# Holding back filler products in a state space stage: every gate block queued behind a step's output products

## The chip, the cores and the metric

The kernel runs on one core of a Trainium2 chip. The metric is the device time of one execution in microseconds (us). A core has TensorE (PE in the profile; its weight loads are PEld), VectorE (DVE), ScalarE (ACT), GpSimd (POOL) and SyncE (SP), each with a queue of its own that it works through in order, and DMA queues. The ones used here are issued by SP, ScalarE and GpSimd.

## The reference

Two layers of a streaming encoder over 2048 prompt positions and 8 x 16 sample positions, 1024 wide. Layer 0 is a diagonal complex state space mixer (S5), layer 1 a gated delta rule mixer. The change lies in layer 0:

```python
proj = h @ w_in
u, z = jnp.split(proj, 2, axis=-1)
...
# 64 groups of 16 channels, 64 complex states each
br = jnp.einsum('gpc,btgc->btgp', bbr, uc)
bi = jnp.einsum('gpc,btgc->btgp', bbi, uc)
...                                  # x_t = Abar x_{t-1} + Bbar u_t, state carried
y = jnp.einsum('gcp,btgp->btgc', c_re, xr) - jnp.einsum('gcp,btgp->btgc', c_im, xi)
...
y = jax.nn.gelu(y + d.astype(F32) * uf)
y = y * jax.nn.sigmoid(y @ w_glu.astype(F32) + b_glu.astype(F32))
y = y * jax.nn.silu(z.astype(F32))
return y.astype(h.dtype) @ w_out, hr, hi
```

The gate z is used only behind the whole scan, so its product with the second half of `w_in` may be computed at any time until then.

## The kernel before, in words

All 2176 positions stand in 8 column tiles of 272. A float32 product is made as three reduced-precision products of a high and a low part (`mm3`, L149 to L151), 24 matmuls for one output block of 128 x 272. Four stages matter here.

1. The projection to u (tile pd), which also leaves h in memory (`h0_d`).
2. The state space stage, 16 steps b, each for 4 groups. `s5_setup(b)` makes the step's matrices on VectorE, with transpositions (abT, L682) and small products (pk, L698) on TensorE. `s5_main(b)` makes input products (pb, L735, two sets of 8 matmuls), turns them (f, z) and scans them (L749) on VectorE, turns the states back (t, xs, L763 to L766), splits them into a high part on ScalarE (xsh, L129) and a low part on VectorE (xsl, L130), and makes the output products py. For each of two halves pl there are two PSUM tiles, py_0 and py_1 for the first, py_2 and py_3 for the second: a Toeplitz product each (L775) and six products with the states each (L780). The L780 products read 64 rows: one tile's use the upper half of TensorE's rows, the other's the lower half (`tile_position`). ScalarE applies the activation to y and stores it (`y_d`).
3. The gate blocks: 64 calls of `z_block`, block n being row block cb = n % 8 of column tile j = n // 8. Each makes one `mm3` into one of two PSUM buffers (pdz), which ScalarE copies out (evz, L630) and stores. Their input is read back from `h0_d` (hz), half a column tile at a time, and split into hhz on ScalarE and hlz on VectorE. They stand in the code behind the 16 steps.
4. The next stage, which loads y (yc), splits it (yh, yl), loads and splits the weights wg (into the buffers of the gate's weights), and makes pg.

The order of each engine's queue isn't the order of the code. A scheduler builds it: an instruction that is ready may stand ahead of code that waits, so gate blocks fill TensorE's time between the steps' products. Two things bind it: data and buffers, and `issue_after`, which the helper `later` uses: instructions traced under it stand, in the queue of the named instruction's engine, behind that instruction. `s5_main` returns `ends`, the last output matmul of each half. Before, only the blocks from 58 on are bound: block 58 to the first half of step 15, blocks 59 to 63 to the second.

Of the kernel before, what the change touches and what calls it, by code (L numbers as in the profile page):

```python
# [41 lines left out]
def bc(ap, axis, n):  # L42
    a = ap.unsqueeze(axis)
    shape = list(a.shape)
    shape[axis] = n
    return a.broadcast_to(shape)


def dram_ap(t, offset, dims):
    return bass.AP(t.tensor, t.offset + offset, [list(d) for d in dims])  # L50
# [3 lines left out]
def kernel(ctx: ExitStack, tc: tile.TileContext, I, O, upto="Z"):  # L54
# [73 lines left out]
    def split_w(dst_hi, dst_lo, raw, lo_eng=None):  # L128
        S.copy(dst_hi, raw)  # L129
        (lo_eng or V).tensor_sub(dst_lo, raw, dst_hi.bitcast(F32))  # L130
# [9 lines left out]
    def later(ins):  # L140
        st = ExitStack()
        for i in ins:
            st.enter_context(tc.issue_after(i))
        return st
# [462 lines left out]
    zst = {"n": 0}  # L607
# [11 lines left out]
    def z_block():  # L619
        j, cb = divmod(zst["n"], 8)  # L620
        zst["n"] += 1
        if cb == 0:
            zst["cur"] = zst.pop("next")
        if cb == 2 and j < 7:
            zst["next"] = load_h0(j + 1)
        hh, hl = zst["cur"]
        ps = psd.tile([P, NCH], F32, tag="d", name=f"pdz{j}_{cb}")
        mm3(ps, ks(wz_hi[cb]), ks(wz_lo[cb]), hh, hl)
        o = ev.tile([P, NCH], F32, tag="o", name=f"evz{j}_{cb}")
        S.copy(o, ps)  # L630
        nc.scalar.dma_start(z_d[j][cb], o)
# [3 lines left out]
    with ExitStack() as pb:  # L635
# [28 lines left out]
        def s5_setup(b):  # L664
            sp = b3.tile([P, SPW], F32, tag="sp", bufs=2, name=f"sp_{b}")
            nc.sync.dma_start(sp, sp_d[b])
            pw = sp[:, PWO:BBO].rearrange("p (l r n) -> p l r n", l=2, r=3)
            bbv = sp[:, BBO:BDO].rearrange("p (r l c) -> p r l c", r=2, l=2)
            bdv = sp[:, BDO:CCO].rearrange("p (r l m) -> p r l m", r=2, l=2)
            ccv = sp[:, CCO:SPW].rearrange("p (r l c) -> p r l c", r=2, l=2)  # L670

            abt = b1.tile([P, 2, 2, 8, 16], F32, tag="abt", name=f"abt{b}")
            tt = b1.tile([P, 2, 2, 9, 16], F32, tag="tt", name=f"abtt{b}")
            for l in range(2):
                V.tensor_mul(abt[:, l], bc(bc(bbv[:, 0, l], 1, 8), 1, 2), bc(pw[:, l, 0:2, 0:8], 3, 16))
                V.tensor_mul(tt[:, l, :, 0:8], bc(bc(bbv[:, 1, l], 1, 8), 1, 2), bc(pw[:, l, 1:3, 0:8], 3, 16))
            V.tensor_add(abt.rearrange("p l r n c -> p (l r) (n c)"), abt.rearrange("p l r n c -> p (l r) (n c)"),
                         tt.rearrange("p l r n c -> p (l r) (n c)")[:, :, 0:128])
            ab = b2.tile([P, 4, P], F32, tag="ab", name=f"ab{b}")
            pt = ps_t.tile([P, 4, P], F32, tag="t", name=f"abT{b}")  # L680
            for q in range(4):
                T.transpose(pt[:, q, :], abt[:, q // 2, q % 2].rearrange("p n c -> p (n c)"), ident)  # L682
            S.copy(ab, pt)

            ca = b3.tile([P, 2, 2, 9, 16], F32, tag="ca", bufs=2, name=f"ca{b}")
            t2 = b1.tile([P, 2, 2, 9, 16], F32, tag="tt", name=f"cat{b}")
            for l in range(2):
                V.tensor_mul(ca[:, l], bc(bc(ccv[:, 0, l], 1, 9), 1, 2), bc(pw[:, l, 1:3], 3, 16))
                V.tensor_mul(t2[:, l], bc(bc(ccv[:, 1, l], 1, 9), 1, 2), bc(pw[:, l, 0:2], 3, 16))
            V.tensor_sub(ca, ca, t2)  # L690
            cs_ = [b2.tile([P, 2, 2, P], F32R, tag="ca" + i, name=f"ca{i}{b}") for i in "hl"]
            split_w(*(t.rearrange("p l r (n c) -> p (l r) n c", c=16) for t in cs_),
                    ca[:, :, :, 1:9].rearrange("p l r n c -> p (l r) n c"))

            pk = ps_t.tile([P, P], F32, tag="t", name=f"pk{b}")
            for l in range(2):
                for r in range(2):
                    T.matmul(pk[32 * l:32 * l + 32, :], lhsT=bdv[:, r, l],  # L698
                             rhs=ca[:, l, r, 0:8, :].rearrange("p n c -> p (n c)"), start=(r == 0), stop=(r == 1),
                             tile_position=(0, 32 * l))  # L700
            kp = b2.tile([64, 240], F32, tag="kp", bufs=1, name=f"kp{b}")
            G.memset(kp[:, 0:112], 0.0)
            S.copy(kp[:, 112:240], pk[0:64])
            V.scalar_tensor_tensor(kp[:, 112:128], dmask, d16[:, b:b + 1], kp[:, 112:128], op0=ALU.mult, op1=ALU.add)
            nc.scalar.dma_start(k_d[b], kp)
            toe = b2.tile([P, 4, P], F32, tag="toe", name=f"toe{b}")
            for g in range(4):
                nc.sync.dma_start(toe[:, g, :], dram_ap(k_d[b], 16 * g * 240, [[16, 8], [240, 16], [1, P]]))
            return cs_, ab, toe

        def s5_load(b):
            u = b2.tile([P, 4, NCH], F32, tag="ur", name=f"u{b}")
            nc.sync.dma_start(u.rearrange("p g c -> p (g c)"),
                              dram_ap(u_d[b // 2], 4 * (b % 2) * NCH, [[8 * NCH, P], [1, 4 * NCH]]))
            tw = b2.tile([P, 2, 2, SEG], F32, tag="tw", name=f"tw_{b}")
            nc.sync.dma_start(tw, tw_d[b])
            return u, tw

        def s5_main(b, u, tw, ca, ab, toe):
# [67 lines left out]
                    y.rearrange("p g c -> p (g c)"))  # L787
            return ends

        par = s5_setup(0)  # L790
        ld = s5_load(0)
        for b in range(16):
            nxt = (s5_load(b + 1), s5_setup(b + 1)) if b < 15 else None
            ends = s5_main(b, *ld, *par)
            if nxt:
                ld, par = nxt
        V.tensor_sub(fsp[:, :, 0], fe[:, 0, :, 0], fe[:, 1, :, 1])
# [8 lines left out]
            zst["next"] = load_h0(0)  # L806
        while zst["n"] < 64:

            with later([ends[zst["n"] > 58]] if zst["n"] > 57 else []):
                z_block()  # L810
    pab.close()
    if upto == "B":
# [472 lines left out]
    with pd:  # L1285
# [457 lines left out]
        par = es.tile([P, 2], F32, name="par")  # L1743
# [329 lines left out]
def _build(arrays, upto="Z"):  # L2073
    import concourse.bacc as bacc

    nc = bacc.Bacc("TRN2", target_bir_lowering=False, num_devices=1)
    I = {k: nc.dram_tensor("in_" + k, v.shape, F32, kind="ExternalInput").ap() for k, v in arrays.items()}
    O = {k: nc.dram_tensor("out_" + k, s, F32, kind="ExternalOutput").ap() for k, s in _OSHAPE.items()}
    with tile.TileContext(nc, schedule_with_timeline_sim=True) as tc:
        dbg = kernel(tc, I, O, upto)  # L2080
    return nc, dbg
# [9 lines left out]
```

## Time and profile before

| what | value |
|---|---|
| three runs | 2153.47, 2156.33, 2158.28 us; median 2156.33 |
| the profiled execution | 2155.81 us |
| its span | 2154.1 us |
| PE busy | 2087.0 us, 97% |
| DVE busy | 1566.3 us, 73% |
| ACT busy | 972.4 us, 45% |
| POOL busy | 476.7 us, 22% |
| pdz matmuls | 512 each of three kinds, first start 272.2, last 619.1 |
| py matmuls | first start 289.9, last 602.4 |

A row of the timeline has the start in us, the length, the engine, line, operation, tiles (output<-inputs), shape and count; what stands in brackets is the engine's idle time before it and what ended that. A row of a window has for each engine the busy us and, in parentheses, the number of instructions that touch the window, then the granted TensorE clock (PEclk, 1.00 is full speed), the share of DMA time and the rate. A row of a group ends with its busy us, the mean length in ns, and the idle time before. A row of waits has total, number and longest.

### The profile page before, as it was taken

The numbers are of one execution on the slowest core, as the hardware profiler recorded it, in microseconds if no ns is written. First come the engines' busy times: TensorE is split into PE (matmuls) and PEld (weight loads), VectorE is DVE, ScalarE is ACT, GpSimd is POOL, SyncE is SP. The second block draws the span as 40 slices with busy tenths as digits, with TensorE's granted clock in tenths as the row PEclk, the third lists the DMA queues.
The fourth block names the chain that finished last, engine by engine and source line by source line (L and its number), as shares of the span: only waits on it lengthen the run. The fifth ranks groups of instructions, "written<-read, shape, count | busy, mean of one in ns | idle before, by whom it ended". The sixth has DMA issues, their size and how long they took to land. (4 is left out here: it accounts for less than half of the span.)

```text
span 2154.1 us, 42178 instructions
## 1 busy us (share of the span) xinstructions
PE 2087.0 (97%) x15729; PEld 1852.0 (86%) x15729; DVE 1566.3 (73%) x4013; ACT 972.4 (45%) x2289; POOL 476.7 (22%) x725
## 2 busy tenths in 40 slices
PE   6999999999889999999999999999999899999998
PEld 4889888888689999999888879889987788888887
DVE  7999598999856554446765669688556888888875
ACT  3543333333255444446665422341224556666663
POOL 1157510000113222222100000100011343444430
PEclk8999999999889999999999999999999899999999
DMA  9697844454284333336465313653456644444432
GB/s 278 238 307 242 250 146 133 145 172 145 93 242 136 126 111 109 110 99 213 139 204 173 93 48 86 163 145 101 137 165 217 195 141 134 124 139 147 146 112 69
DMA packets 395209, 332.40 MB, mean 154 GB/s; under 512 B 88026, under 2 KB 358890, under 8 KB 395004
## 3 DMA queue, kind: packets, MB, share of 16 engines
q1 hardware_dynamic: 259084, 226.56, 35.3%
q10 hardware_dynamic: 133104, 95.49, 13.8%
q0 software_dynamic: 2816, 7.65, 1.0%
q8 instruction: 124, 2.03, 0.4%
q14 instruction: 81, 0.66, 0.1%
HBM read 213.01 MB, written 116.61 MB: 153 GB/s over the span
## 5 line engine op out<-in xcount | busy, mean ns | idle before, releaser
L149 PE MATMUL pc<-h1h,wdh 128*128 128x512 f32 (+1 forms) x600 | 216.5, 361 | 0.1
L151 PE MATMUL pc<-h1h,wdl 128*128 128x384 f32 (+1 forms) x600 | 214.9, 358 | 0.0
L150 PE MATMUL pc<-h1l,wdh 128*128 128x384 f32 (+1 forms) x600 | 214.8, 358 | 0.1
L1404 DVE SCALAR_TENSOR_TENSOR ac<-pb,convw,ac 128x384 f32<-128x384 f32 (+3 forms) x288 | 163.5, 591 | 3.3
L150 PE MATMUL pdz<-hlz,wzh 128*128 128x272 f32 x512 | 152.4, 298 | 0.0
L149 PE MATMUL pdz<-hhz,wzh 128*128 128x272 f32 x512 | 151.6, 297 | 0.7 <-ACT evz L630 0.7
L149 PE MATMUL pg<-yh,wgh 128*128 128x272 f32 x512 | 148.2, 289 | 3.5 <-ACT evz L630 3.5
L151 PE MATMUL pdz<-hhz,wzl 128*128 128x272 f32 x512 | 150.9, 295 | 0.0
L149 PE MATMUL po<-gh,woh 128*128 128x272 f32 x512 | 148.2, 290 | 1.4 <-ACT gh L937 1.4
L150 PE MATMUL pg<-yl,wgh 128*128 128x272 f32 x512 | 149.1, 291 | 0.0
L151 PE MATMUL pg<-yh,wgl 128*128 128x272 f32 x512 | 148.2, 290 | 0.0
L151 PE MATMUL po<-gh,wol 128*128 128x272 f32 x512 | 147.9, 289 | 0.0
L150 PE MATMUL po<-gl,woh 128*128 128x272 f32 x512 | 147.1, 288 | 0.0
L149 PEld LDWEIGHTS pc<-h1h,wdh 128*128 128x128 f32 x600 | 112.6, 188 | 12.4 <-issue 1.7
L150 PEld LDWEIGHTS pc<-h1l,wdh 128*128 128x128 f32 x600 | 112.7, 188 | 10.4 <-issue 0.8
L151 PEld LDWEIGHTS pc<-h1h,wdl 128*128 128x128 f32 x600 | 112.6, 188 | 10.2 <-issue 0.8
L149 PE MATMUL pd<-hh,wuh 128*128 128x272 f32 x384 | 112.7, 294 | 0.1
L69 PE MATMUL epo<-w2h,ohi 128*128 128x512 f32 x272 | 111.5, 410 | 0.0
L150 PE MATMUL pd<-hl,wuh 128*128 128x272 f32 x384 | 110.8, 289 | 0.3 <-DVE hl L230 0.3
L151 PE MATMUL pd<-hh,wul 128*128 128x272 f32 x384 | 110.9, 289 | 0.0
L69 PE MATMUL epo<-w2h,olo 128*128 128x512 f32 x272 | 106.9, 393 | 0.0
L69 PE MATMUL epo<-w2l,ohi 128*128 128x512 f32 x272 | 106.8, 393 | 0.0
(617 smaller groups left out, 6334.5 us busy)
## 6 DMA issues: line engine op xcount, KB each, us to landing
wa<-in_w_ada SPq DMA_DIRECT2D x32, 512.0 KB
wdr<-in_w_in SPq DMA_DIRECT2D x24, 512.0 KB
h_d<-x ACTq DMA_DIRECT2D x8, 1088.0 KB
u_d<-ev ACTq DMA_DIRECT2D x64, 136.0 KB
hz<-h_d SPq DMA_DIRECT2D x16, 544.0 KB
u<-u_d SPq DMA_DIRECT2D x16, 544.0 KB
z_d<-evz ACTq DMA_DIRECT2D x64, 136.0 KB
y_d<-y ACTq DMA_DIRECT2D x32, 272.0 KB
```

Of the source, the lines that this page charges most:

```text
L69: i_ = f(*a, **kw)
L149: T.matmul(ps, lhsT=w_hi[k], rhs=x_hi[k], start=(k == 0), stop=False)
L150: T.matmul(ps, lhsT=w_hi[k], rhs=x_lo[k], start=False, stop=False)
L151: i_ = T.matmul(ps, lhsT=w_lo[k], rhs=x_hi[k], start=False, stop=(k == n - 1))
L1404: V.scalar_tensor_tensor(o, src(j), convw[:, b, j:j + 1], o, op0=ALU.mult, op1=ALU.add)
```

## The change

The last matmuls of all steps are kept, 32 in number (index 2b + pl), and each gate block is bound to one of them:

```diff
+        ends = []
         par = s5_setup(0)
         ld = s5_load(0)
         for b in range(16):
             nxt = (s5_load(b + 1), s5_setup(b + 1)) if b < 15 else None
-            ends = s5_main(b, *ld, *par)
+            ends += s5_main(b, *ld, *par)
             if nxt:
                 ld, par = nxt
...
         while zst["n"] < 64:
 
-            with later([ends[zst["n"] > 58]] if zst["n"] > 57 else []):
+            n = zst["n"]
+            step = 2 * (n * 15 // 52) - 1 if n < 52 else 29 if n < 58 else 30 + (n > 58)
+            with later([ends[step]] if step > 0 else []):
                 z_block()
```

Blocks 0 to 3 are free. Blocks 4 to 51 go 3 or 4 each behind the second half of steps 0 to 13, blocks 52 to 57 behind that of step 14, and the last six stay as they were. Names below carry the number of the step (py5_2), or of column tile and row block (pdz0_4 is block 4, pdz7_0 is block 56).

TensorE's queue from the second input product of step 0 on, before:

```order
L735 MATMUL pb0_1_4217<-u0_4153,ab0_4120 64x272 x4
L150 MATMUL pdz0_4_6407<-hlz0_0_6274,wzh4_4026 128x272
L698 MATMUL pk1_4188<-ca1_4177,sp_1_4161 32x128 x4
L775 MATMUL py0_0_4252<-u0_4153,toe0_4148 128x272
L775 MATMUL py0_1_4253<-u0_4153,toe0_4148 128x272
L151 MATMUL pdz0_4_6407<-hhz0_0_6273,wzl4_4027 128x272
```

and in the changed kernel:

```order
L735 MATMUL pb0_1_4217<-u0_4153,ab0_4120 64x272 x4
L775 MATMUL py0_0_4252<-u0_4153,toe0_4148 128x272
L698 MATMUL pk1_4188<-ca1_4177,sp_1_4161 32x128 x4
L775 MATMUL py0_1_4253<-u0_4153,toe0_4148 128x272
L682 MATMUL abT2_4305<-ident_160,abt2_4297 128x128 x4
L735 MATMUL pb1_0_4342<-u1_4157,ab1_4170 64x272 x4
L698 MATMUL pk2_4322<-ca2_4311,sp_2_4295 32x128 x4
L682 MATMUL abT3_4439<-ident_160,abt3_4431 128x128 x4
L735 MATMUL pb1_1_4351<-u1_4157,ab1_4170 64x272 x4
L780 MATMUL py0_0_4252<-xsh0_4247,cah0_4134 128x272
```

The gate blocks are gone from here until step 0's last output product (160 gate matmuls stood in this stretch before).

TensorE's queue at the second half of step 5's output products, before:

```order
L775 MATMUL py5_2_4942<-u5_4693,toe5_4734 128x272
L775 MATMUL py5_3_4943<-u5_4693,toe5_4734 128x272
L780 MATMUL py5_2_4942<-xsh5_4917,cah5_4720 128x272
L780 MATMUL py5_3_4943<-xsh5_4917,cah5_4720 128x272
L780 MATMUL py5_2_4942<-xsl5_4918,cah5_4720 128x272
L780 MATMUL py5_3_4943<-xsl5_4918,cah5_4720 128x272
```

and in the changed kernel:

```order
L775 MATMUL py5_2_4942<-u5_4693,toe5_4734 128x272
L780 MATMUL py5_2_4942<-xsh5_4917,cah5_4720 128x272
L780 MATMUL py5_2_4942<-xsl5_4918,cah5_4720 128x272
L780 MATMUL py5_2_4942<-xsh5_4917,cal5_4721 128x272
L780 MATMUL py5_2_4942<-xsh5_4917,cah5_4720 128x272
L780 MATMUL py5_2_4942<-xsl5_4918,cah5_4720 128x272
L780 MATMUL py5_2_4942<-xsh5_4917,cal5_4721 128x272
L775 MATMUL py5_3_4943<-u5_4693,toe5_4734 128x272
L780 MATMUL py5_3_4943<-xsh5_4917,cah5_4720 128x272
```

The two tiles' products no longer alternate. It is so in steps 0, 2 to 12 and 14 (in step 11 for the first five); before it was so in step 14 alone.

ScalarE's queue behind step 15's last activation, before:

```order
L785 DMA y_d_119<-y15_1_6235 128x544
L631 DMA z_d7_78<-evz7_2_8016 128x272
L135 CAST wgh3_8176<-wgr3_8254 128x1024
L630 COPY evz7_3_8044<-pdz7_3_8019 128x272
L631 DMA z_d7_78<-evz7_3_8044 128x272
L900 CAST yh0_0_8232<-yc0_0_8230 128x1088
L630 COPY evz7_4_8072<-pdz7_4_8047 128x272
```

and in the changed kernel:

```order
L230 CAST hhz7_1_7763<-hz7_1_7761 128x1088
L785 DMA y_d_119<-y15_1_6235 128x544
L630 COPY evz6_7_7932<-pdz6_7_7907 128x272
L631 DMA z_d6_77<-evz6_7_7932 128x272
L903 CAST yh0_0_8232<-yc0_0_8230 128x1088
L135 CAST wgh0_8182<-wgr0_8242 128x1024
L630 COPY evz7_0_7960<-pdz7_0_7935 128x272
L903 CAST yh0_1_8238<-yc0_1_8236 128x1088
```

The cast of y and that of the first weights now stand ahead of the copy of block 56 (evz7_0), and a split of the gate's input ahead of y's last store.

## The prediction

> **What bounds the kernel now.** I read the page first, for the engines by slice.
>
> ```profile
> span 2154.1 us, 42178 instructions
> PE   6999999999889999999999999999999899999998
> PEclk8999999999889999999999999999999899999999
> ```
>
> TensorE (PE) is full nearly everywhere, so its time is the kernel's: work that it doesn't do in a hole must be done later. The change lies in the state space stage, so I cut that stage by windows at the landmarks: z blocks begin (272.19), the fourth block ends (287.10), the products of step 0 end (318.92), the z blocks that may run ahead are used up (568.38), the first half of step 15's products ends (595.95), step 15 ends (602.69), the next stage begins (622.91).
>
> ```profile
> core 0: us, PE busy (x) PEld busy (x) DVE busy (x) ACT busy (x) POOL busy (x), PEclk, DMA share, GB/s
> 287.10:318.92 31.82, 31.82 (x254) 27.26 (x252) 31.13 (x75) 10.51 (x24) 0.48 (x3) 1.00 0.40 121
> 318.92:568.38 249.46, 248.04 (x1901) 205.67 (x1901) 223.01 (x469) 86.54 (x215) 3.63 (x25) 1.00 0.46 146
> 568.38:595.95 27.57, 16.31 (x66) 9.91 (x64) 23.68 (x37) 4.74 (x11) 7.42 (x8) 0.58 0.26 89
> 595.95:602.69 6.74, 6.74 (x41) 6.15 (x39) 2.45 (x2) 2.67 (x4) 0.00 (x0) 0.69 0.69 191
> 602.69:622.91 20.22, 15.97 (x124) 15.38 (x123) 7.79 (x7) 9.94 (x15) 0.00 (x0) 1.00 0.83 250
> ```
>
> Up to 568 PE has no idle time to speak of (248.04 of 249.46); VectorE has some (223.01). From 568.38 to 595.95 there is no z block left for PE: a hole, and a granted clock of 0.58. The same windows for the z blocks' tile alone:
>
> ```profile
> 287.10:318.92 31.82, 22.88 (x162) 20.52 (x160) 2.71 (x7) 1.00 0.40 121
> 318.92:568.38 249.46, 164.17 (x1136) 146.17 (x1136) 18.14 (x47) 1.00 0.46 146
> 568.38:595.95 27.57, 0.16 (x2) 0.00 (x0) 0.39 (x1) 0.58 0.26 89
> 602.69:622.91 20.22, 15.97 (x122) 15.38 (x122) 2.27 (x6) 1.00 0.83 250
> ```
>
> A z block is 24 matmuls. Their price is the distance between starts, not the listed length, since they overlap; these are 22 rows apart:
>
> ```profile
> 609.12 0.28 PE L150 MATMUL pdz<-hlz,wzh 128*128 128x272 f32 x1
> 611.87 0.29 PE L151 MATMUL pdz<-hhz,wzl 128*128 128x272 f32 x1
> ```
>
> So 2.75 / 22 = 0.125 us each, 3.0 us a block. In the long window 1136 of them are 142 us; the other 106 us are 13 steps of state space work, 8.1 us of PE each. VectorE is busy 223.01 / 13 = 17.2 us a step.
>
> **The change, term by term.** No instruction is added; 60 of 64 z blocks wait in PE's queue for a step's products. I keep a ledger of PE time up to the next stage's first matmul (after it PE is full, and a shift there stays).
>
> *(a) The late hole is filled: a gain.* What PE does from 568.38 to 595.95 at full clock: the products of step 14 in part, two input products of step 15, half of step 15's output products. Full clock prices, and the half-clock rows for the form that exists only there:
>
> ```profile
> L735 PE MATMUL pb<-u,ab 128*64 128x272 f32 x208 | 32.2, 406 | 1.4 <-DMA u<-u_d 1.4
> 565.20 1.08 PE L775 MATMUL py<-u,toe 128*128 128x272 f32 x4
> 566.21 0.39 PE L780 MATMUL py<-xsh,cah 64*128 64x272 f32 x2
> 567.15 0.39 PE L149 MATMUL pdz<-hhz,wzh 128*128 128x272 f32 x1
> 578.11 0.43 PE L780 MATMUL py<-xsh,cal 64*128 64x272 f32 x2
> 578.33 0.43 PE L780 MATMUL py<-xsh,cah 64*128 64x272 f32 x2
> 579.70 1.27 PE L775 MATMUL py<-u,toe 128*128 128x272 f32 x2 [0.48 <-ACT y L784]
> 581.30 0.42 PE L780 MATMUL py<-xsl,cah 64*128 64x272 f32 x1
> 581.52 0.42 PE L780 MATMUL py<-xsh,cal 64*128 64x272 f32 x1
> 585.42 2.18 PE L775 MATMUL py<-u,toe 128*128 128x272 f32 x4
> ```
>
> A group of 8 input products is 32.2 / 26 = 1.2; two Toeplitz products 566.21 - 565.20 = 1.01; twelve output products in pairs 567.15 - 566.21 = 0.94; the pair in single file 585.42 - 579.70 = 5.72 at half clock, so 2.86. Sum 1.01 + 2 x 1.2 + 0.94 + 2.86 + 1.01 + 0.94 = 9.2 of 27.57: 18.4 lost. Then the clock stays low:
>
> ```profile
> 594.52 0.60 PE L780 MATMUL py<-xsl,cah 64*128 64x272 f32 x2 [0.73 <-DVE xsl L130]
> 595.95 0.59 PE L149 MATMUL pdz<-hhz,wzh 128*128 128x272 f32 x1
> 599.74 0.43 PE L150 MATMUL pdz<-hlz,wzh 128*128 128x272 f32 x1
> 600.17 0.29 PE L149 MATMUL pdz<-hhz,wzh 128*128 128x272 f32 x1
> 600.67 1.08 PE L775 MATMUL py<-u,toe 128*128 128x272 f32 x4
> ```
>
> 22 z matmuls take 600.67 - 595.95 = 4.7 instead of 2.75: 2.0 more. In the changed order blocks 52 to 55 fill these steps, so (a) = -20.4.
>
> *(b) An early hole opens: a loss.* Blocks 4 and on now stand behind step 0's products. Before, PE did 160 z matmuls between 287.10 and those products' end (162 records touch that window, two at its edges), 160 x 0.125 = 20.0 us. Now it has only the state space work there, which VectorE paces:
>
> ```profile
> 308.31 1.28 DVE L130 TENSOR_TENSOR xsl<-xs,xsh 128x1088 fp32r<-128x1088 f32 x1
> 318.85 0.39 PE L150 MATMUL pdz<-hlz,wzh 128*128 128x272 f32 x1
> ```
>
> VectorE is busy 31.13 of 31.82 there and its order up to this row is nearly unchanged (one split leaves, smaller work for step 4 comes in front), so I leave 309.6. Behind it stand five pairs (595.95 - 594.52 = 1.43 at half clock), a transposition (about 1.0) and the single file (5.72). PE, mostly idle since 291, will be at half clock, and by the last rows comes back 600.17 - 594.52 = 5.6 us after steady work begins: to 315.2 half clock, the remaining 2.5 at full clock in 1.3, end 316.5 instead of 318.85. (b) = 20.0 - 2.35 = +17.6. Bounds: all at full clock 313.9, so 15; all at half and z matmuls slow behind it, 21. The Trainium skill (TensorE: Matmul & The Clock Gate, "Part 1: The HAM clock gate") puts the return at about 3.4 us of sustained work; by that figure the end, an estimate, is 315.4 and the total 1.1 us less; the row is longer, and I take the row.
>
> *(c) The single file: a loss.* In steps 2 to 12 the second pair of output products is no longer interleaved (py_2, py_3, py_2, ...) but runs py_2 whole, then py_3; before, only step 14 had this. In pairs, two matmuls on opposite halves of the rows start together (x2 rows, 0.22 apart at half clock); alone, one takes the same 0.22. So 12 slots for 6, and the Toeplitz products split: 2.86 against 1.01 + 0.94 = 1.95, 0.91 a step, 11 steps: +10.0. Bounds: slots alone 6 x 0.12 = 0.72, so 7.9; 11 above. It isn't hidden: a step now has 84 z matmuls on average, 10.5 + 8.1 + 0.9 = 19.5 us of PE against VectorE's 17.2. What waits there is VectorE, as before:
>
> ```profile
> DVE f L740 <- ACT bs L738: 22.7, 10, 4.5
> ```
>
> *(d) The end of the stage.* Behind step 15 now stand 206 z matmuls instead of 122; that is work moved, already in the ledger. But ScalarE's queue there is reordered: block 56's eviction stands behind a cast of y for the next stage, which waits for y's store and load.
>
> ```profile
> 603.56 0.33 ACTq L785 DMA_DIRECT2D y_d<-y  x1
> 607.48 0.92 SPq L895 DMA_DIRECT2D yc<-y_d  x2
> 611.46 1.10 ACT L900 CAST yh<-yc 128x1088 fp32r<-128x1088 f32 x1 [4.07 <-DMA yc<-y_d]
> 614.72 1.05 ACT L135 CAST wgh<-wgr 128x1024 fp32r<-128x1024 f32 x1 [0.38 <-DMA wgr<-in_w_glu]
> 612.89 0.39 PE L149 MATMUL pdz<-hhz,wzh 128*128 128x272 f32 x1 [0.73 <-ACT evz L630]
> 622.91 0.39 PE L149 MATMUL pg<-yh,wgh 128*128 128x272 f32 x1 [3.52 <-ACT evz L630]
> ```
>
> Let E be step 15's end. The store is issued at E + 1.9 (0.7 of activation, then a cast of the same shape as the yh row's, 1.1, that now stands ahead of it), the load 3.9 later, the cast 4.0 after that: E + 9.8; two casts (1.10, 1.05) and the eviction (0.4) end at E + 12.1. PE is through 62 matmuls at E + 7.8 and needs that buffer: 4.3 idle, 2.0 of slow clock, 0.4 for the last eviction: 6.7. Before: 0.73 + 3.5, and 2.0 slow: 6.3. (d) = +0.4; from -4 (the load is early) to +5 (each weight load late). The queues of SP and GpSimd carry the same DMAs; SP's weight loads 2 to 7 move behind y's loads, which costs what (d) has.
>
> Sum: -20.4 + 17.6 + 10.0 + 0.4 = +7.6. The profiled execution took 2155.81 us (span 2154.1), 0.5 under the median 2156.33; 2155.8 + 7.6 = 2163.4.
>
> **Rivals.** *Single file costs nothing* (c = 0), if one row half's matmuls run at the pairs' pace. Then step 0's products also end near 314.9, (b) = 16.0, and the sum is -4.0: 2151.8, the other side. It decides below 0.37 us a step. For it: single file was seen once, at half clock. Against it: the rows at 581.30 and 578.11 show the same slot for one as for two. The Trainium skill (TensorEngine Tiling (Array Packing), "Key Properties") has different tiles in parallel, and a drain at each change of mode, for which it gives no price; the row at 579.70 agrees with a cost.
> *Both holes come out small*: the front keeps full clock, (b) = 15.0, and y's load is 4 us early: -20.4 + 15.0 + 10.0 - 3.6 = +1.0, 2156.8. Against: 0.58 was granted in the late hole, with as little work.
> *The end stalls more*: the weight casts, each waiting for its load in ScalarE's queue, hold each eviction behind them by 1 us or so, five times: (d) = +5.4, 2168.4. For it: casts that waited for loads in the rows above.
>
> **Chances.** About 0.2% (4.3 us) is what a measurement of this kernel can tell. Forecast 0.57, rival one 0.15, two 0.13, three 0.15. Slower: most of the forecast (0.48) and rival three, 0.64 with a little of two; within 0.2%: the forecast's low edge, most of rival two, part of one, 0.24; faster 0.12. Range 2152 to 2171, from rival one's time to three's with (b) at 20.
>
> **What would show it.** After: no z matmul between 287 and about 316, and a low clock there; z matmuls throughout steps 14 and 15; L780 rows x1 in eleven steps and 0.9 us more from py_2's Toeplitz row to the end; PE idle some 4 us before an eviction behind step 15. Wrong if step 0's products end well before 314, if the single file takes under 2.3 us at full clock, or if PE idles within the steps.

## The result, and the profile after

The changed kernel takes 2172.74 us (median of 4 runs, 2169.41 to 2175.31) against 2155.9 for the kernel before, measured beside it: ratio 1.0074, 95% interval [1.0062, 1.0086], or 16.8 us more. The forecast was 2163.4, at most 2171: the sign was right, the size too small.

The page after, span, TensorE (PE) by slice and its granted clock:

```profile
span 2170.5 us, 42186 instructions
PE   6999979999999999999999999999999899999998
PEclk9999979999999999999999999999999899999999
```

The hole has moved: the 7 stands in the sixth slice (271 to 326 us), and the two 8s of before, in the eleventh and twelfth, are gone. Next, windows at the landmarks of the prediction (the same columns hold for every such row below): fourth gate block done, products of step 0 end (316.18), step 1 ends (334.27), step 13 ends (569.31), step 15 ends (605.54), the next stage begins (635.03).

```profile
core 0: us, PE busy (x) PEld busy (x) DVE busy (x) ACT busy (x) POOL busy (x), PEclk, DMA share, GB/s
286.60:316.18 29.58, 16.37 (x94) 9.77 (x93) 29.44 (x73) 6.75 (x17) 0.67 (x4) 0.69 0.25 67
316.18:334.27 18.09, 18.09 (x118) 15.14 (x120) 12.55 (x24) 4.56 (x13) 0.11 (x1) 0.85 0.31 103
334.27:569.31 235.04, 234.46 (x1713) 192.49 (x1713) 207.86 (x437) 81.12 (x197) 3.37 (x23) 1.00 0.47 146
569.31:605.54 36.23, 34.16 (x252) 29.34 (x251) 27.29 (x47) 9.72 (x23) 7.47 (x8) 1.00 0.42 134
605.54:635.03 29.49, 26.27 (x206) 25.83 (x206) 11.26 (x10) 13.69 (x21) 0.00 (x0) 1.00 0.66 202
```

In the first row PE is busy 16.37 of 29.58 us, VectorE (DVE) 29.44. Over the 18 us behind it the granted clock is 0.85 on average. From 334 to 569 PE has 0.58 us of idle time and VectorE 27: PE sets the length of these steps, which is the condition under which a dearer step costs time.

The second pair of output products of step 5, in the timeline of the changed kernel:

```profile
410.57 0.72 PE L775 MATMUL py<-u,toe 128*128 128x272 f32 x2
411.23 0.39 PE L780 MATMUL py<-xsh,cah 64*128 64x272 f32 x1
411.46 0.29 PE L780 MATMUL py<-xsl,cah 64*128 64x272 f32 x1
411.59 0.28 PE L780 MATMUL py<-xsh,cal 64*128 64x272 f32 x1
...
411.96 0.28 PE L780 MATMUL py<-xsh,cal 64*128 64x272 f32 x1
412.18 0.73 PE L775 MATMUL py<-u,toe 128*128 128x272 f32 x2
...
413.78 0.39 PE L149 MATMUL pdz<-hhz,wzh 128*128 128x272 f32 x1
```

Single file, at full clock: 413.78 - 410.57 = 3.21 us. A half-array matmul alone takes a slot of 0.125, what a pair took before. Of the 1.26 over the pairs' 1.95, only 0.75 is slots (6 x 0.125). The rest lies at the changes of form, of which there are now twice as many: two Toeplitz matmuls take 0.66, twice, where all four took 1.01 (0.31 more), and one slot more behind a Toeplitz product and one more ahead of the next are 0.22 to 0.23 instead of 0.125 (0.2).

### The profile page after: what moved, and what is told of

Read it like the earlier page. It is cut to its first block, busy times and chain, and to the rows that moved or that the text cites. A ratio compares the mean times of both kernels' runs of the same rounds, so it can differ in the third digit from the quotient of the medians.

```text
span 2170.5 us, 42186 instructions
## 1 busy us (share of the span) xinstructions
PE 2098.4 (97%) x15729; PEld 1859.5 (86%) x15729; DVE 1566.7 (72%) x4013; ACT 974.1 (45%) x2289; POOL 476.3 (22%) x725
## 5 line engine op out<-in xcount | busy, mean ns | idle before, releaser
L149 PEld LDWEIGHTS pc<-h1h,wdh 128*128 128x128 f32 x600 | 112.7, 188 | 13.1 <-ACT pb L1396 1.8
L937 POOL TENSOR_TENSOR zt<-zt,sz 128x272 f32<-128x272 f32 x64 | 62.4, 978 | 202.7 <-ACT sz L936 202.7
```

The lines of the kernel that those rows point to most:

```text
L149: T.matmul(ps, lhsT=w_hi[k], rhs=x_hi[k], start=(k == 0), stop=False)
L937: G.tensor_mul(zt, zt, sz)
```

## The experiments

All but one were measured over three or five rounds beside the kernel before. A ratio is against the kernel before in the same rounds (medians 2153.6 to 2156.1). "Next stage" is the start of its first matmul (pg) in the profiled execution.

| kernel | gate blocks | second pair | median us | ratio [95%] | next stage |
|---|---|---|---|---|---|
| before | 58 free | interleaved but in step 14 | 2155.9 | 1 | 622.91 |
| change | 4 free, spread | single file | 2172.74 | 1.0074 [1.0062, 1.0086] | 635.03 |
| 1 | 4 free, spread | interleaved | 2157.25 | 1.0006 [0.9997, 1.0016] | 624.62 |
| 2 | 4 free, rest behind step 0 | interleaved | 2158.43 | 1.0023 [1.0010, 1.0035] | 623.12 |
| 3 | 11 free, 41 spread | interleaved | 2154.66 | 0.9996 [0.9985, 1.0007] | 618.95 |
| 4 | 58 free | interleaved, bound | 2155.36 | 1.0001 [0.9989, 1.0013] | 623.62 |
| 5 | the change again | single file | 2172.11 | 1.0075 [1.0056, 1.0093] | 636.19 |
| 6 | 4 free, spread | single file in steps 7 to 12 and 14 | 2162.84 | 1.0028 [1.0015, 1.0040] | 628.22 |
| 7 | 11 free, 49 spread | interleaved | 2144.92 | 0.9950 [0.9933, 0.9967] | 612.04 |
| 8 | as 3 | single file | 2155.33 | 0.9997 [0.9981, 1.0012] | 618.17 |
| 9 | 58 free | single file, bound | 2168.74 | 1.0061 [1.0042, 1.0079] | 633.68 |
| 10 | before again | interleaved | 2157.19, one run | - | 621.02 |
| 11 | 11 free, 48 spread | interleaved | 2151.99 | 0.9977 [0.9965, 0.9989] | 612.84 |
| 12 | as 7 | interleaved | 2143.64 | 0.9949 [0.9935, 0.9962] | 611.48 |

**1. The gates of the change, the pairs interleaved.** TensorE's instructions of the output products are bound to the order in which they are written:

```diff
             for pl in range(2):
+                T.ordered, T.last = True, None
                 y = b2.tile([P, 2, NCH], F32, tag="y", name=f"y{b}_{pl}")
...
                 ends.append(i_.ins)
+                T.ordered = False
```

> The changed kernel with one thing undone: the output products of each half of a step are bound in the order of the code, so py_2 and py_3 alternate in all steps as py_0 and py_1 do; the gate blocks stay where the change put them (96 matmuls before the end of step 0's products, 1329 before step 15's). Theory A, TensorE's ledger: single file costs TensorE time that nothing hides, 3.21 us for the two tiles in the changed trace against 1.95 interleaved, 1.26 a step, and 12 more steps than before have it (0, 2 to 12): 15 us less than the changed kernel, 2172.7 - 15 = 2157.7, if step 0's, which lies in the front hole, counts too; 2159 if not. Theory B, VectorE paces the steps: single file is hidden behind VectorE's 17.2 us a step, and the time stays within 2 us of 2172.7.

2157.25, as theory A had it: with the gates where the change puts them, giving back the interleaving takes back 15.5 of the 16.8 us (step 14's pair is interleaved here too, which the expectation doesn't count). Windows of this kernel at the same landmarks as those after the step-0 row above (step 0 ends at 316.21, step 1 at 331.85, step 13 at 557.79):

```profile
316.21:331.85 15.64, 15.64 (x118) 12.72 (x120) 12.54 (x24) 4.85 (x14) 0.11 (x1) 1.00 0.35 117
331.85:557.79 225.94, 222.57 (x1715) 184.91 (x1715) 206.94 (x438) 79.30 (x197) 3.35 (x23) 1.00 0.49 152
```

The long stretch is 9.1 us shorter than in the changed kernel with the same gate blocks in it (two matmuls more), and PE now has 3.4 us of idle time there, against 0.58: some of what the single file costs would have been idle time. And 118 matmuls behind step 0 take 15.64 at full clock instead of 18.09 at 0.85, which the prediction had in its upper bound alone.

**2. The front hole alone.** With the edit of 1:

```diff
-            step = 2 * (n * 15 // 52) - 1 if n < 52 else 29 if n < 58 else 30 + (n > 58)
+            step = -1 if n < 4 else 1 if n < 58 else 30 + (n > 58)
```

> The kernel before with interleaving bound in all steps and one part of the change: blocks 4 to 57 stand behind step 0's products and nothing else; no quota for the later steps. Theory A: the front hole costs 17.3 us and some 2.7 us of slow clock behind it, but the 160 gate matmuls that it displaces are then left to fill the late hole (121 matmuls remain behind step 15, as before): +20 - 20, so within 3 us of before, 2153 to 2159. Theory B, TensorE's holes cost nothing where VectorE paces: the front hole is free and the filled late hole is a gain of 15 or more, 2141 or less.

2158.43, inside A's range: the front hole that opens and the late hole that closes nearly cancel, whether or not the blocks are spread. In this execution the products of step 0 ran at full clock and ended at 313.87 (the prediction's lower bound was 313.9), so the front cost 15.0 us by the ledger, and the last two steps gave back 14.0.

**3. The front left open.** With the edit of 1:

```diff
+            step = -1 if n < 11 else 2 * ((n - 11) * 14 // 41) + 1 if n < 52 else 29 if n < 58 else 30 + (n > 58)
```

> The changed kernel with interleaving bound and the front hole closed: blocks 0 to 10 are free (256 gate matmuls before the end of step 0's products, as in the kernel before), blocks 11 to 51 go 3 each (2 to 4) behind steps 0 to 13, the rest as in the change; 169 remain behind step 15. Theory A: 15 us less than the changed kernel for the interleaving and 20 for the front, 2138; with 72 gate matmuls a step TensorE has 9.0 + 8.1 = 17.1 us a step, no more than VectorE's 17.2, so TensorE will wait in the steps and some of the gain is lost: 2138 to 2147. Theory B, where the front hole is free: the same as the interleaved kernel, 2158 by A's price or 2172 by B's own.

2154.66: a miss. The front stayed full (step 0's products end at 318.26, with all 256 gate matmuls), and yet the ledger has lost 12.7 us by the end of step 13. Windows of this kernel, steps 1 to 13 and one piece of them:

```profile
318.26:557.08 238.82, 226.37 (x1709) 184.75 (x1709) 219.66 (x463) 81.14 (x205) 3.63 (x25) 0.98 0.47 146
400.00:415.00 15.00, 12.25 (x68) 9.12 (x68) 12.18 (x30) 5.33 (x12) 0.29 (x2) 0.66 0.51 160
```

With three gate blocks a step PE idles 12.4 us of 238.8; from 400 to 415 a wait of 1.4 us and three of 0.4 to 0.5 stand beside a granted clock of 0.66. Neither engine is full in the stretch (VectorE is busy 219.66), and which waits set the length of the steps was not worked out. Another 169 gate matmuls, 21 us, are left behind step 15, more than y's way to memory and back has to cover (6.4 us in the changed kernel, from the store's issue at 606.28 to the cast at 612.67).

**4. Before, with the binding of 1 alone.**

```diff
+            step = -1 if n < 58 else 30 + (n > 58)
```

> The kernel before with interleaving bound in all steps: only step 14 had single file there. A control for the binding itself. Theory A: 1 to 2 us less in the late hole at half clock, where VectorE sets the end: 2154 to 2156. Theory B: 2156. If the binding costs something of its own, it shows here.

2155.36: the binding itself, with step 14's pairs now interleaved, costs or gains nothing that the measurement can tell (the interval is some 2.6 us to either side).

**5. The change once more**, for a second profile.

> The changed kernel once more, as it stands, for a second profile. In the first one the shift against the kernel before was 12.3 us at the start of the next stage's second group of products and 16.5 us at the end: some 4 us were lost behind the stage, where the change edits nothing. Theory V (variation between executions): this profile shows another figure behind the stage, between -1 and +3 us, and the median stays 2170 to 2175. Theory S (the order behind the stage is really worse): it shows 4 us again, within 1 us, at the same places (two waits on ScalarE at 1028 to 1070, and the last stage). Both expect step 0's products to end at 316 to 317 and 3.2 us for the second pair of output products in steps 2 to 12.

The median repeats (2172.11). Behind the stage theory V holds: from the next stage's start to the end this execution took 2.3 us less than the first. But in the stage both expectations missed one thing: step 0's products ended at 318.15, not 316 to 317, because all of their single file ran at half clock. Run 10 belongs here: before, once more.

> The kernel before once more, for a second profile. Seven of the nine other profiles took 0.8 to 4.8 us longer than the first profile of before from the start of the next stage to the end, where no edit reaches. Theory V (that first profile was short there by chance): this one takes 1 to 4 us more in that part. Theory S (the orders behind the stage differ): within 0.5 us of the first.

The next stage starts 1.9 us earlier than in the first profile of before, the span ends 1.3 later: 3.2 us more behind the stage, V again. So single profiles of this kernel differ by 2 to 3 us within a part, and a term below that size can't be read from one of them.

**6. Half of the steps interleaved.**

```diff
+                T.ordered, T.last = b < 7, None
```

> The change with the second pair of output products interleaved again in steps 0 to 6 alone (their order of creation kept); steps 7 to 12 stay in single file (14 as before). Theory A: the single file costs 1.26 us a step (3.21 against 1.95 us, as the changed kernel's trace has it), each step the same: 6 x 1.26 = 7.6 us above the fully interleaved kernel's 2157.3, so 2164.8 (2163 to 2167). With the predicted 0.91 a step it would be 2162.7. Rival B: the loss sits in the front of the stage (step 0's single file at low clock sets off the rest): 2157 to 2160, all of it gone.

2162.84, between: under A's range by 0.2 and near the 0.91 figure, and 5.6 above kernel 1 for six steps. By the ends of the steps, corrected for gate matmuls at 0.125 each, kernel 6 loses 5.5 us on kernel 1 from step 7 to step 12, as much as the changed kernel does there (5.6): these six steps cost the same in both, some 0.9 each, net of kernel 1's idle time. The rest of the loss lies in the steps ahead, so rival B's "all of it gone" falls too.

**9. The single file alone**, on the gates of before:

```diff
+                one = pl == 1 and 2 <= b <= 12
...
+                for i in range(2 if one else 0):
+                    T.matmul(pys[i], lhsT=toe[:, 2 * pl + i], rhs=u[:, 2 * pl + i], start=True, stop=False)
+                    for r in range(2):
+                        for wi, xi in ((0, 0), (0, 1), (1, 0)):
...
+                            i_ = T.matmul(pys[i], lhsT=ca[wi][ln, pl, r], rhs=xs[xi][ln, pl, r],
...
```

> The kernel before with one part of the change alone: in steps 2 to 12 the second pair of output products in single file, the gates as before (all other pairs interleaved as created). Theory A: TensorE has no idle time in these steps (248.04 busy of 249.46 us), so 11 steps at 1.1 to 1.26 us come on top: 12 to 14 us above the kernel with the same gates interleaved (2155.4), so 2167 to 2170. With the predicted 0.91 it is 2165.4. Rival B: what made the change slow is single file together with the gates' new places; alone it is hidden by the z blocks that run ahead: 2155 to 2159.

2168.74, 13.4 above kernel 4: A, and the larger price. Without any change of the gates the order of one pair in eleven steps costs 13 us. The window of its steps 1 to 13:

```profile
318.58:577.92 259.34, 258.86 (x1900) 214.28 (x1900) 223.31 (x464) 86.83 (x214) 3.64 (x25) 1.00 0.45 140
```

PE full (0.5 idle), VectorE busy as before: nothing there to hide it.

**8. The single file where TensorE is not the bound**: the gates of 3, without the edit of 1.

> Blocks 0 to 10 free, 11 to 51 three a step behind steps 0 to 13, the rest as in the change; the second pair of output products in single file, in 13 steps. Against the same kernel interleaved (2154.7). Theory A: the single file costs only where TensorE sets the step's length. Here a step has 72 gate matmuls, 9.0 + 8.1 + 1.26 = 18.4 us of TensorE against the 18.5 us that VectorE took a step in that kernel, so nearly all of it is hidden: 2154 to 2160. Rival B: the products are on the chain from VectorE's scan to the next step, or TensorE is the bound anyway: 13 x 1.26 = 16.4 us more, 2171.

2155.33 against 2154.7: no cost that can be told from the scatter (the intervals are 2 to 3 us to either side), where 16.4 would be seen. The same stretch as the first row for 3, then a piece of kernel 3's own:

```profile
317.91:557.21 239.30, 234.01 (x1710) 190.40 (x1709) 220.22 (x469) 82.82 (x206) 3.64 (x25) 1.00 0.47 147
403.81:414.05 10.24, 9.40 (x47) 7.14 (x43) 7.82 (x21) 2.37 (x7) 0.29 (x2) 0.50 0.65 198
```

PE is busy 7.6 us longer than in 3 and the stretch is 0.5 longer, while VectorE's work is the same: PE's idle time fell from 12.4 to 5.3. That holds about half of the price of some 15 us in these twelve steps. Another 4 us or so are the 10 us at half clock that 3 had (the second row) and this execution, the shortest of its kernel (2148.97), had not (an estimate: 9.40 us busy, by the factor of 1.8 between 5.72 and 3.21 us for the same single file at half and at full clock). So it is the medians, of ten runs each, that carry the answer. With 9 they settle it: the price is paid where PE has no idle time, and not here, where it has.

**7, 11, 12. The front open and fewer blocks left for the end.** With the edit of 1; 7 and 12 are the same kernel:

```diff
+            step = -1 if n < 11 else 2 * ((n - 11) * 15 // 49) + 1 if n < 60 else 31
```

> Interleaved, blocks 0 to 10 free (so nothing is taken out of the front), 11 to 59 three or four each behind steps 0 to 14, the last four behind step 15. Theory A (the ledger): the kernel with 11 free blocks and ten behind step 14 and 15 (2154.7) left 169 gate matmuls, 21 us, behind the last step while VectorE paced the steps at 18.5 us; here 78 a step, 9.8 + 8.1 = 17.9 us of TensorE, still fit under VectorE's 18.5, and 96 are left (12 us, about the 10 to 12 us that y's store and load take): the next stage starts at 604 to 609 instead of 619, and the time is 2140 to 2146. Rival B: TensorE and VectorE no longer fit together, since each step's products wait for VectorE and hold the gate blocks queued behind them; the steps get longer by what leaves the end: 2150 to 2156.

> As the kernel with blocks 11 to 59 spread over steps 0 to 14, with five blocks behind step 15 instead of four and 11 to 58 spread. There TensorE stood idle 3.6 us ahead of the next stage. Theory A (that idle time waits for the evictions and weight casts behind y's load, some 13 us behind the step's end): 24 more gate matmuls fill 3.0 us of it, and the steps get shorter by part of that: 0.5 to 3 us less than 2144.9. Rival B: VectorE sets the step's end, and the idle time follows the last eviction wherever it is: 2144 to 2148.

> The kernel with blocks 11 to 59 spread over steps 0 to 14 and four behind step 15, once more in more rounds. It measured 2144.9 (2140.1 to 2149.7), its neighbour with five blocks behind step 15 measured 2152.0 (2145.0 to 2154.1), though TensorE's ledger has the neighbour no slower. Theory A (the difference between the two is real, idle time within the steps at low clock): 2142 to 2148 again. Rival B (both scatter over some 9 us from execution to execution, by where TensorE's short waits let the clock fall, and seven runs fell low by chance): 2147 to 2152. Both expect it below the kernel before.

Kernel 7 is the fastest: 2144.92, inside A's range, though its next stage starts at 612.04 and not at 604 to 609. Measured again it took 2143.64, in A's range and not in rival B's; both are 0.5% under before. Of what 3 left behind step 15, 73 matmuls moved into the steps. Windows of it (the first of the two profiles, of its longest run, 2149.66), steps 1 to 13, the last two, and the end:

```profile
318.78:558.84 240.06, 235.02 (x1799) 194.99 (x1798) 219.79 (x463) 82.21 (x208) 3.64 (x25) 0.99 0.47 148
558.84:595.53 36.69, 32.56 (x232) 27.44 (x232) 28.62 (x46) 11.44 (x25) 7.49 (x8) 0.95 0.36 114
595.53:612.04 16.51, 12.74 (x97) 12.10 (x97) 6.57 (x6) 8.11 (x12) 0.00 (x0) 1.00 0.97 291
```

90 matmuls more than in 3 fit into steps 1 to 13 for 1.2 us more: PE idles 5.0 there, not 12.4. Behind step 15 it still waits 3.6 us for the last eviction. Kernel 11, with one block more for that wait, should have been no slower and was 2151.99: both theories missed. Its next stage starts only 0.8 later than 7's; its steps 4 and 5 lost 3.4 and 2.4 us against 7's, and the clock fell there and again in step 15, as two windows of it show:

```profile
389.00:397.00 8.00, 5.52 (x30) 4.11 (x31) 6.10 (x14) 2.82 (x6) 0.18 (x1) 0.65 0.55 177
591.00:598.00 7.00, 6.05 (x32) 4.86 (x33) 2.45 (x2) 3.71 (x7) 0.00 (x0) 0.63 0.80 239
```

Most of that was won back in step 6, and this execution is one of 11's shorter ones (2146.0), while that of 7 is its longest, so the 7 us between the medians of 7 and 11 are not explained by them and stay open.

## Why the prediction came out too small, by its own steps

The ledger again, with the two profiles of the changed kernel against the first of before; shifts of step ends, with 0.125 us for each gate matmul that is ahead in one and not in the other.

| term | predicted | profile 1 | profile 2 |
|---|---|---|---|
| (b) front, to the end of step 1 | +17.6 | +18.8 | +20.5 |
| (c) steps 2 to 13 | +10.0 | +11.2 | +11.2 |
| (a) steps 14 and 15 | -20.4 | -16.6 | -16.6 |
| (d) end of the stage | +0.4 | -1.2 | -1.8 |
| start of the next stage | +7.6 | +12.1 | +13.3 |
| behind it | 0 | +4.4 | +2.0 |
| span | +7.6 | +16.5 | +15.3 |

The experiments part the loss in another way. Without the single file the prediction had -4.0 us (its first rival), and kernel 1, which has the gates' places alone, measured +1.3. So the prediction gave the single file 11.6 us of its sum, and the change takes 15.5 more than kernel 1. Both parts were forecast too small, by 5.3 and 3.9.

**(a) is the term that was mis-sized most: 16.6, not 20.4.** The step that failed is "blocks 52 to 55 fill these steps". The two last steps in windows of the gate tile alone (length, PE, weight loads, ScalarE, clock, DMA share, GB/s), before:

```profile
567.21:602.69 35.48, 6.28 (x32) 5.83 (x32) 0.39 (x1) 0.62 0.36 113
```

and after:

```profile
569.31:605.54 36.23, 23.90 (x171) 21.88 (x171) 2.70 (x7) 1.00 0.42 134
```

139 more in 0.75 us more: 139 x 0.125 - 0.75 = 16.6. The clock did come back to 1.00 as forecast. But step 15 ends with VectorE's scans, and the blocks that stand ahead of its products run out before them, as the timelines of VectorE and TensorE after show:

```profile
595.87 0.68 DVE L766 TENSOR_TENSOR xs<-t 128x510 f32<-128x510 f32 x1
...
597.79 0.39 PE L780 MATMUL py<-xsh,cah 64*128 64x272 f32 x2 [1.58 <-ACT xsh L129]
```

PE idles 2.07 of the 36.23 (1.58 of it here, 0.48 ahead of step 14's second pair). A further 0.35 is step 14's single file, 3.21 us at full clock where I had halved its half-clock row to 2.86. The rest, 1.4, fits the price of 0.125, which leaves out the changes of form: without the wait, 170 gate matmuls of these two steps take 22.96 us from start to start, 1.7 more than 170 x 0.125, about what their places next to matmuls of another form cost, where one takes 0.23 and not 0.125 (589.01 to 589.24, right behind step 14's last product). The other kernels that fill the two steps got 12.2 (11) to 18.5 (8) out of them, by the same ledger, and none the 20.4: a hole that ends with another engine's chain wasn't worth its length.

**(b) was right about the hole and short at its edge.** No gate matmul runs from 287 to 316, the clock is 0.50 from 294.33 to 311.40, and step 0's products end at 316.18, forecast 316.5. That they agree so well is luck: the forecast had half clock to 315.2 and full clock behind it, and this execution had full clock up to 314.8 and half behind it; in the second profile they ended at 318.15. What failed is that nothing slow was put behind them; only the upper bound had it. Windows of 2 us, of the changed kernel:

```profile
312.00:314.00 2.00, 1.65 (x9) 1.14 (x9) 1.97 (x10) 0.58 (x2) 0.19 (x1) 1.00 0.27 100
314.00:316.00 2.00, 2.00 (x9) 1.50 (x8) 1.97 (x5) 0.41 (x2) 0.00 (x0) 0.70 0.33 74
316.00:318.00 2.00, 2.00 (x9) 1.90 (x9) 2.00 (x3) 1.11 (x3) 0.00 (x0) 0.50 0.86 288
318.00:320.00 2.00, 2.00 (x11) 1.88 (x9) 2.00 (x5) 0.58 (x1) 0.00 (x0) 0.50 0.88 275
```

and of kernel 1:

```profile
314.00:316.00 2.00, 2.00 (x14) 1.41 (x12) 1.97 (x5) 0.00 (x0) 0.00 (x0) 0.50 0.50 88
316.00:318.00 2.00, 2.00 (x16) 1.86 (x15) 2.00 (x3) 1.41 (x4) 0.00 (x0) 0.91 0.70 259
```

In the changed kernel the clock came back ahead of the single file and fell again in the middle of it, and the gate matmuls behind started 0.226 apart until 321.6. In kernel 1 the interleaved pairs end at the same time and the clock is full from then on. Step 0's single file so cost 2.4 us at the end of step 1 in this profile and 4.1 in the second, both against kernel 1. The return after about 3.4 us of sustained work that the Trainium skill gives (TensorE: Matmul & The Clock Gate, "Part 1: The HAM clock gate") is near what kernel 1 shows, where the products begin at 312.37 and the clock is back at 316.35, 4.0 us on; in the changed kernel work is as unbroken from 312.35, and the clock, up already, falls at 314.8 and is back for good at 321.6, 9 us on, so there, with the single file taken as work, the measurement goes against the page's figure, and against my 5.6 too. The last section shows that the single file counts for less.

**(c) was nearly right by a wrong price.** By the rows the single file costs 3.21 - 1.95 = 1.26 a step and not 0.91: I halved the half-clock time, but 5.72 at half clock is 3.21 at full: a factor of 1.8, not 2. Step 5's row is one of the dearest: the eleven places take 2.96 to 3.21 against 1.96, 13.1 in all, which is about what the single file costs alone (13.4, kernel 9). The ledger shows 11.2 of it in the stretch; 0.8 of the difference is idle time that before had there (1.42 in the prediction's window, now 0.58), the other 1.1 I did not find.

**(d) had the right places and a small error.** The cast of y starts at 612.67 behind a wait of 4.75, and the eviction of block 56 behind it. Rows of the timelines of ScalarE and TensorE after:

```profile
612.67 1.10 ACT L903 CAST yh<-yc 128x1088 fp32r<-128x1088 f32 x1 [4.75 <-DMA yc<-y_d]
613.68 1.04 ACT L135 CAST wgh<-wgr 128x1024 fp32r<-128x1024 f32 x1
614.62 0.38 ACT L630 COPY evz<-pdz 128x272 f32<-128x272 f32 x1
...
615.05 0.39 PE L149 MATMUL pdz<-hhz,wzh 128*128 128x272 f32 x1 [1.55 <-ACT evz L630]
...
635.03 0.39 PE L149 MATMUL pg<-yh,wgh 128*128 128x272 f32 x1 [1.68 <-ACT evz L630]
```

The store was issued 0.7 us after the step's end, not 1.9 (the cast that stands ahead of it started at 606.13, the issue followed at 606.28), and the eviction was over 9.5 us after it, not 12.1 (the prediction's own terms, 9.8 + 1.10 + 1.05 + 0.4, make 12.35). So PE waited 1.55 and not 4.3, and the clock stayed at 1.00; the last eviction held it 1.68 instead of 0.4.

**Behind the stage** I had put nothing, and 2.0 to 4.4 us lie there by the first profile of before; by its second (next stage at 621.02, end at 2155.4) it is -1.2 to +1.1, and the stage itself 14.0 and 15.2 us worse. So the place of 2 to 4 us of the loss, ahead of that start or behind it, changes with the execution compared; the sum stays between 14.0 and 16.5 over the four pairs of profiles.

**The rivals.** "Single file costs nothing" is false here (kernels 1 and 9), and true where TensorE has idle time (kernel 8). "Both holes come out small" had its first half in kernel 2 (full clock in the front, 15.0), not in the changed kernel. "The end stalls more" did not come.

## What to carry to other kernels

Before moving fill work, look at what the scheduler does to the order of the work it moves past: here the gates' places were worth +1.3 us (interval -0.6 to +3.4) and the broken pairing of half-array matmuls 15.5. A price on an engine counts only where that engine paces the stretch: the same single file cost 13 us in a kernel with TensorE at 100% of the stretch and nothing that could be told in one with it at 95%. In these runs fill work was best taken from where it covered nothing (blocks left behind the last step) and not from where it already covered a wait, and a hole that ends with another engine's chain gave back less than its length.

## What was unexpected of the hardware

The granted clock fell from 1.00 to 0.50 while TensorE worked without a pause and half-array matmuls ran one at a time (314.8 in the changed kernel), and stayed at half for some 5 us of full-array matmuls behind them. It did so in one of two executions; in the other it had not risen at all. In the kernels with that pair interleaved it was full from 316.35 (1) and 317.09 (6) on, and in kernel 2 from 310.86.

A rival cause is the wait of 1.08 us just ahead (it ends at 312.35). Kernel 2 has the same wait (1.09 us, to 311.74), also with the clock up, and its pair interleaved. In the changed kernel the clock changed at 294.33, 311.40, 314.81 and 321.64, whole multiples of 3.41 us apart, so the windows below are cut on that grid, each kernel's own; the second of each two shows what was granted next. First come the changed kernel and kernel 2:

```profile
311.40:314.81 3.41, 2.46 (x11) 1.59 (x12) 3.38 (x14) 1.57 (x4) 0.19 (x1) 1.00 0.27 93
314.81:318.22 3.41, 3.41 (x15) 3.16 (x15) 3.38 (x5) 1.12 (x3) 0.00 (x0) 0.50 0.69 203
...
310.86:314.27 3.41, 2.53 (x19) 1.94 (x20) 3.38 (x14) 1.58 (x4) 0.18 (x1) 1.00 0.43 106
314.27:317.69 3.42, 3.42 (x28) 3.34 (x27) 3.39 (x5) 1.23 (x5) 0.00 (x0) 1.00 0.71 258
```

Then, with the clock still down and no idle time in the first row of each, the changed kernel's second profile (5) and kernel 1:

```profile
312.81:316.22 3.41, 3.41 (x10) 1.96 (x9) 3.38 (x10) 0.40 (x1) 0.00 (x0) 0.50 0.23 84
316.22:319.63 3.41, 3.41 (x14) 2.95 (x14) 2.40 (x4) 1.12 (x3) 0.00 (x0) 0.50 0.56 164
...
312.94:316.35 3.41, 3.41 (x17) 2.29 (x16) 3.38 (x9) 0.32 (x1) 0.00 (x0) 0.50 0.49 120
316.35:319.76 3.41, 3.41 (x27) 3.41 (x28) 3.41 (x7) 1.31 (x5) 0.00 (x0) 1.00 0.81 255
```

With nearly the same idle time the clock falls behind the single file and stays up behind the pairs; with none it stays down behind the single file and comes up behind the pairs. So the wait alone is not the cause, and a half-array matmul by itself counted for less than a pair, both in holding the clock and in raising it. That rests on one execution each, and no kernel was made to test it. That the clock was already up in two of these executions and down in two, behind the same work, fits the place of the grid: PE was busy 3.28 us of 307.99:311.40 in the changed kernel and 3.20 of 307.45:310.86 in kernel 2, but only 2.34 of 309.52:312.94 in kernel 1, where the wait fell into the stretch, and of 309.39:312.81 in 5. At full clock in steps 2 to 12 the same single file, with gate matmuls around it, never lowered the clock.
